# A one-core decoder trunk step: the S5 steps dealt out over nearly the whole body, and two attention-branch units ahead of the gated unit

## The chip, the cores and the metric

The kernel runs on one core of a Trainium2 chip. The metric is device time in microseconds (us) of one execution, the median of three runs. The core's engines each run a queue of their own in order: TensorE (PE, matrix products; PEld is its loading of weights), VectorE (DVE), ScalarE (ACT), GpSimd (POOL) and SyncE (SP), which here issues the transfers between the chip's main memory and the core's on-chip memory. Engines wait for each other by semaphores.

## The reference, cut

One layer of a hybrid decoder, for 256 prompt tokens and 8 x 8 sample tokens that share the weights; the kernel carries all 320 tokens together.

```python
h = rmsnorm(x)
z = h @ w_in                     # S5 input | GLA q, k, v, gate, forget | memory q | 3 x merge gates
y_s5, s5_state   = s5(u_s5)      # diagonal complex state space, scan over time, then
                                 # y = gelu(y);  y = y * sigmoid(y @ w_glu + b_glu)
y_gla, gla_state = gla(q, k, v, r, a_low, s0)   # 4 heads, chunked; per-head rmsnorm; * silu(r)
y_x              = memory_attention(q_x, mem_k, mem_v)   # 4 heads, 256 memory tokens
merged = gate0 * (y_s5 @ w_br_s5) + gate1 * (y_gla @ w_br_gla) + gate2 * (y_x @ w_br_xattn)
x = x + merged @ w_out
x = x + swiglu(rmsnorm(x))
y = rmsnorm(x)                   # returned with the new states and the memory's k and v
```

## The kernel before, in words

Every weight matrix is read in units of 128 x 2048 fp32 (1 MB). A unit is loaded by SP into one of three `raw` buffers (L70), rounded by ScalarE to `whi` (L82), and VectorE takes the remainder `wlo` (L83); both have two buffers. Activations are split in the same way into a high and a low part. `mm3` (L95) then makes three products for each block of 128 rows: high x high (L99), high x low (L100), low x high (L101), 48 matmuls of 128x320 in a unit. The names ending in h and l are such pairs: `hh, hl` the normed input, `yxh, yxl` the attention branch's output, `ygh, ygl` the GLA's, `ysh, ysl` the gated S5's, `y1h, y1l` the S5 output ahead of its gate.

The program has three stages. `front` norms the input and projects the memory (to about 100 us). `body` (L1082) makes the products with `w_in` and everything that hangs on them, and `back` (L1127) makes the merge, the output projection and the feed-forward part.

`body` runs three streams of steps, written as generators: `main` (four attention heads, then `IDLE` empty steps, `gla_setup` at L846, then four GLA heads, `gla` at L888), `s5` (eight tiles of the S5 scan: products `bu` at L658, tables and scans on VectorE up to L704, products `yp` at L713), and `gates` (48 units whose results go to `d_gate` by L1079). A stream has a number of steps and of units, `STEPS`, and an end, `ENDS`: its pace is (steps + units) / end, and the loop at L1110 always takes the stream that is furthest behind by its pace. So `ENDS` says at which share of the body a stream is done. Before, S5 has 0.8.

A GLA head ends as follows, and the places named below lie here. For each half of the sample tokens, SP loads four states into `gl_s` (L1016; one buffer), TensorE multiplies them (L1020), ScalarE copies (L1025), TensorE transposes (L1028), VectorE adds into `gl_o` (L1032), makes masked values `gl_vr` (L1040), TensorE multiplies (L1043), VectorE updates the states (L1046), and SP stores them (`o_gs`, L1050). After the second half: L1055, the head's sum of squares (L1061, L1062), its inverse root (TensorE L134, VectorE L142 to L154, TensorE L162), the scaling of `gl_o` (L1064), two units for the output gate (`gl_sr`, stored to `d_r`, L1070), and the store of the head to `d_yg` (L1072).

`back` first loads the attention output in four pieces (`yraw<-d_yx`, L1141, two buffers `yraw`) and splits them into `yxh, yxl` (L1124, L1125), then the GLA output (`yraw<-d_yg`, with `yr<-d_r`, L1147 to L1151) into `ygh, ygl`. The gated unit (GLU) comes next: four units of `w_glu` on `y1h, y1l`, which need the end of S5. Then `branch(m2, bi)` takes a unit of `w_br` for output pair m2 and branch bi (2 attention, 1 GLA, 0 S5): load of the gates `gld`, 48 matmuls, products with the gates into `macc`. The order before is (0,2), (1,2), (0,0), (1,0), (0,1), (1,1), then for each m2 from 2 to 7 the branches 2, 1, 0.

A scheduler turns this into one queue for each engine, so that steps of different streams, and of body and back, stand between each other on an engine; the orders shown below are those queues.

Of the kernel before, what the change touches and what calls it, by code (L numbers as in the profile page):

```python
# [8 lines left out]
F32 = mybir.dt.float32  # L9
F32R = mybir.dt.float32r  # L10
U8 = mybir.dt.uint8
I32 = mybir.dt.int32
AF = mybir.ActivationFunctionType
ALU = mybir.AluOpType
# [4 lines left out]
P = 128  # L19
# [3 lines left out]
NT = NP_ + NS  # L23
# [6 lines left out]
IDLE = 14  # L30
STEPS = (129 + IDLE, 32), (113, 8), (49, 48)
W_PROJ = 1.0
ENDS = (1.0, 0.8, 1.0)
HEADS = 4
FH = 5632
FQ = 4
# [8 lines left out]
C_BGLU, C_GN, C_BA, C_DS = 64, 72, 80, 84  # L45
# [4 lines left out]
class Build:  # L50
# [1031 lines left out]
    def body(self):  # L1082
        def s5():
            self.prepared = self.s5_prep(0)
            yield
            for ut in range(8):
                yield from self.s5_tile(ut, self.prepared)
# [5 lines left out]
        def main():  # L1093
            yield from heads(self.attn)

            for _ in range(IDLE):
                yield
            self.pop(self.left)
            self.pop(self.left)
            self.gla_setup()  # L1100
            yield from heads(self.gla)
# [5 lines left out]
            [it, (steps + W_PROJ * proj) / end, 0]  # L1107
            for it, (steps, proj), end in zip((main(), s5(), self.gates()), STEPS, ENDS)
        ]
# [17 lines left out]
    def back(self):  # L1127
        nc, io = self.nc, self.io
        TT = nc.vector.tensor_tensor
        self.wide = True  # L1130
        yp = self.push(self.left, "y", bufs=1)
# [3 lines left out]
        ys = []  # L1135
        for n, d in (("x", self.d_yx), ("g", self.d_yg)):
            hi = yp.tile([P, 8, NT], F32R, name=f"y{n}h")
            lo = self.low(yp, f"y{n}l", 8)
# [12 lines left out]
                    TT(raw[:], raw[:], r[:], op=ALU.mult)  # L1151
                self.split(hi[:, 2 * c : 2 * c + 2, :], lo[:, 2 * c : 2 * c + 2, :], raw[:])
            ys.insert(0, (hi, lo))
        hi = yp.tile([P, 8, NT], F32R, name="ysh")
        lo = self.low(yp, "ysl", 8)
        gp = self.push(self.right, "glu", bufs=1)
        y1h = gp.tile([P, 8, NT], F32R, name="y1h")
        y1l = self.low(gp, "y1l", 8)
        for c in range(2):
            nc.scalar.activation(  # L1160
                self.y1[:, 4 * c : 4 * c + 4, :], self.y1[:, 4 * c : 4 * c + 4, :], AF.Gelu_apprx_tanh
            )
        for m in range(8):
            self.split(y1h[:, m, :], y1l[:, m, :], self.y1[:, m, :])
        for m2 in range(4):
            wh, wl = self.unit(io["w_glu"][m2])
            for i in range(2):
                m = 2 * m2 + i
                ps = self.psum_mm()
                self.mm3(ps[:, :NT], wh, wl, 8 * i, 8, y1h, y1l)  # L1170
                sg = yp.tile([P, NT], F32, name="glu", tag="glu", bufs=2)
                nc.scalar.activation(sg[:], ps[:, :NT], AF.Sigmoid, bias=self.vec[:, C_BGLU + m : C_BGLU + m + 1])
                TT(sg[:], sg[:], self.y1[:, m, :], op=ALU.mult)
                self.split(hi[:, m, :], lo[:, m, :], sg[:])
        ys.insert(0, (hi, lo))
        gates = self.d_gate[:].rearrange("p (b m) t -> p b m t", b=3)
        self.pop(self.right)
        bp = self.push(self.right, "branch", bufs=1)
        acc = {}

        def branch(m2, bi, last=0):
            wh, wl = self.unit(io["w_br"][bi, m2])
            g = bp.tile([P, 2, NT], F32, name="gld", tag="gld", bufs=3)
            nc.sync.dma_start(g[:], gates[:, bi, 2 * m2 : 2 * m2 + 2, :])
            nc.scalar.activation(g[:], g[:], AF.Sigmoid)
            for i in range(2):
                m = 2 * m2 + i
                ps = self.psum_mm()
                self.mm3(ps[:, :NT], wh, wl, 8 * i, 8, *ys[bi])
                if bi == 2:  # L1190
                    acc[m] = bp.tile([P, NT], F32, name="macc", tag="macc", bufs=4)[:]
                    TT(acc[m], ps[:, :NT], g[:, i, :], op=ALU.mult)
                else:
                    TT(g[:, i, :], ps[:, :NT], g[:, i, :], op=ALU.mult)
                    TT(acc[m], acc[m], g[:, i, :], op=ALU.add)
                    if bi == last:
                        self.split(mh[:, m, :], ml[:, m, :], acc[m])


        for m2, bi in ((0, 2), (1, 2), (0, 0), (1, 0), (0, 1), (1, 1)):  # L1200
            branch(m2, bi, last=1)
        for m2 in range(2, 8):
            for bi in (2, 1, 0):
                branch(m2, bi)
# [25 lines left out]
        for m in range(KD):  # L1230
            wh, wl = self.unit(io["w_out"][m])
            ps = self.psum_mm()
# [13 lines left out]
        for q in range(FQ):  # L1246
            for i in range(FT):
                m = q * FT + i
                wh, wl = self.unit(io["w_fg"][m])
# [6 lines left out]
                wh, wl = self.unit(io["w_fu"][m])  # L1256
# [4 lines left out]
            for m in range(KD):  # L1261
                wh, wl = self.unit(io["w_fd"][q, m], FT * P)
                ps = self.psum_mm()
# [128 lines left out]
```

## Time and profile before

| | us |
|---|---|
| runs (three) | 2089.7, 2090.43, 2091.97; median 2090.43 |
| the profiled execution's own time | 2090.89 |
| its span, first to last instruction | 2089.1 |
| TensorE busy | 2064.1 (99%) |
| VectorE busy | 1290.8 (62%) |
| ScalarE busy | 852.2 (41%) |
| GpSimd busy | 141.2 (7%) |

The profile is one execution, and the time of its rows runs from 0 at the first instruction. Matmuls are pipelined, so the durations of single ones overlap and their starts tell the rate. In a row of a timeline, `[1.50 <-DMA gl_s<-s]` says that the engine was idle for 1.50 us before the instruction, and what ended that. The four GLU units run from 845.8 to 876.9 us, the first unit with `yxh` starts at 876.88.

### The profile page before, as it was taken

Reading aid. Unit: us, or ns where it says so; the run is one execution under the profiler, and the core shown is the slowest. Engines: PE = TensorE matmul, PEld = TensorE weight load, DVE = VectorE, ACT = ScalarE, POOL = GpSimd, SP = SyncE. Lnnn points to the kernel's source line nnn. Section 1 sums busy time; section 2 is a strip of 40 time slices with the busy share of each in tenths; the row PEclk is TensorE's granted clock in tenths of the full one; section 3 lists DMA queues with packets and bytes.
Section 4 is the critical chain, followed back from the end, with each engine's and each line's share of the span. In section 5 each row is a group of like instructions: output and inputs, shape, how many; then the busy total and the mean of one; then the engine's idle time right before and its main releaser. Section 6 shows DMA issues by size and latency. Waiting matters only on the chain.

```text
span 2089.1 us, 33964 instructions
## 1 busy us (share of the span) xinstructions
PE 2064.1 (99%) x14390; PEld 2014.3 (96%) x14390; DVE 1290.8 (62%) x1961; ACT 852.2 (41%) x1121; POOL 141.2 (7%) x181
## 2 busy tenths in 40 slices
PE   9999999999999999999999999999999999999997
PEld 7998998999999999999999999999999999999997
DVE  7977779887997945675555444444444444444445
ACT  7544445554445344544333333233323333333343
POOL 8211011012101000000000000000000000000000
PEclk9999999999999999999999999999999999999998
DMA  9765664445454454766554444454435443454443
GB/s 336 257 233 196 230 219 150 151 151 173 140 180 149 148 197 148 259 216 200 189 196 161 142 144 140 142 180 147 156 125 178 152 151 130 152 178 146 149 135 111
DMA packets 71673, 362.23 MB, mean 173 GB/s; under 512 B 8032, under 2 KB 16096, under 8 KB 41696
## 3 DMA queue, kind: packets, MB, share of 16 engines
q1 hardware_dynamic: 71520, 360.05, 50.3%
q8 instruction: 113, 1.85, 0.4%
q14 instruction: 40, 0.33, 0.0%
HBM read 338.49 MB, written 21.53 MB: 172 GB/s over the span
## 4 chain that ended last, share of the span: by engine, by line
PE 89%; DVE 7%; DMA 1%; issue 1%; ACT 1%; SPq 0%; DVEq 0%; ACTq 0%
PE pmm L101 19%; PE pmm L99 18%; PE pmm L100 18%; PE psm L101 10%; PE psm L99 10%; PE psm L100 9%; DVE wlo L83 2%; DVE s_w L677 1%; DMA o_gs<-gl_s 1%; DMA gl_s<-s 0%; PE psm L954 0%; ACT whi L82 0%; PE psm L805 0%; PE yp L713 0%; PE bu L658 0%
## 5 line engine op out<-in xcount | busy, mean ns | idle before, releaser
L82 ACT CAST whi<-raw 128x2048 fp32r<-128x2048 f32 (+3 forms) x308 | 540.2, 1754 | 931.5 <-issue 528.8
L83 DVE TENSOR_TENSOR wlo<-raw,whi 128x2048 fp32r<-128x2048 f32 (+3 forms) x308 | 646.1, 2098 | 279.5 <-ACT whi L82 277.7
L101 PE MATMUL pmm<-hh,wlo 128*128 128x320 f32 x1408 | 438.6, 311 | 2.9 <-DVE wlo L83 2.8
L99 PE MATMUL pmm<-hh,whi 128*128 128x320 f32 x1408 | 437.2, 311 | 0.0
L100 PE MATMUL pmm<-hl,whi 128*128 128x320 f32 x1408 | 432.3, 307 | 0.0
L99 PEld LDWEIGHTS pmm<-hh,whi 128*128 128x128 f32 x1408 | 265.5, 189 | 5.8 <-issue 5.5
L101 PEld LDWEIGHTS pmm<-hh,wlo 128*128 128x128 f32 x1408 | 264.4, 188 | 6.9 <-DVE wlo L83 3.5
L100 PEld LDWEIGHTS pmm<-hl,whi 128*128 128x128 f32 x1408 | 265.3, 188 | 2.0 <-issue 1.3
L101 PE MATMUL pmm<-fh,wlo 128*128 128x320 f32 x704 | 216.8, 308 | 0.0
L101 PE MATMUL psm<-fh,wlo 128*128 128x320 f32 x704 | 216.8, 308 | 0.0
L99 PE MATMUL psm<-fh,whi 128*128 128x320 f32 x704 | 215.5, 306 | 0.0
L99 PE MATMUL pmm<-fh,whi 128*128 128x320 f32 x704 | 215.5, 306 | 0.0
L100 PE MATMUL pmm<-fl,whi 128*128 128x320 f32 x704 | 213.4, 303 | 0.0
L100 PE MATMUL psm<-fl,whi 128*128 128x320 f32 x704 | 213.3, 303 | 0.0
L99 PEld LDWEIGHTS psm<-fh,whi 128*128 128x128 f32 x704 | 132.2, 188 | 0.1
L100 PEld LDWEIGHTS psm<-fl,whi 128*128 128x128 f32 x704 | 132.2, 188 | 0.0
L100 PEld LDWEIGHTS pmm<-fl,whi 128*128 128x128 f32 x704 | 132.2, 188 | 0.0
L99 PEld LDWEIGHTS pmm<-fh,whi 128*128 128x128 f32 x704 | 132.1, 188 | 0.0
L101 PEld LDWEIGHTS pmm<-fh,wlo 128*128 128x128 f32 x704 | 131.7, 187 | 0.0
L101 PEld LDWEIGHTS psm<-fh,wlo 128*128 128x128 f32 x704 | 131.6, 187 | 0.0
L101 PE MATMUL pmm<-hidh,wlo 128*128 128x320 f32 x352 | 108.9, 309 | 0.2 <-DVE wlo L83 0.2
L101 PE MATMUL psm<-hidh,wlo 128*128 128x320 f32 x352 | 108.4, 308 | 0.0
(448 smaller groups left out, 3648.6 us busy)
## 6 DMA issues: line engine op xcount, KB each, us to landing
raw<-w_in SPq DMA_DIRECT2D x88, 1024.0 KB, 4.9
raw<-w_fg SPq DMA_DIRECT2D x44, 1024.0 KB, 4.8
raw<-w_fu SPq DMA_DIRECT2D x44, 1024.0 KB, 4.8
raw<-w_fd SPq DMA_DIRECT2D x64, 704.0 KB, 4.1
raw<-w_br SPq DMA_DIRECT2D x24, 1024.0 KB, 4.9
at_kv<-kv SPq DMA_DIRECT2D x32, 512.0 KB, 5.7
raw<-w_out SPq DMA_DIRECT2D x16, 1024.0 KB, 4.9
raw<-w_mk SPq DMA_DIRECT2D x8, 1024.0 KB, 6.2
```

Source lines behind the costliest of these rows:

```text
L82: nc.scalar.copy(hi[:, s], raw[:, s])
L83: nc.vector.tensor_tensor(lo[:, s], raw[:, s], hi[:, s].bitcast(F32), op=ALU.subtract)
L99: nc.tensor.matmul(ps, hi[:, ws], xh[:, kx + k, :], start=k == 0, stop=False)
L100: nc.tensor.matmul(ps, hi[:, ws], xl[:, kx + k, :], start=False, stop=False)
L101: nc.tensor.matmul(ps, lo[:, ws], xh[:, kx + k, :], start=False, stop=k == nk - 1)
L677: nc.vector.tensor_tensor_scan(fl[:, c * n : c * n + m], af[:, :m], fl[:, c * n : c * n + m], 0.0, op0=M, op1=A)
```

## The change

Two edits. `ENDS` for the S5 stream goes from 0.8 to 0.93, so that its pace falls and its steps are dealt out over 93% of the body. In `back`, the GLU is put into a function and called after `branch(0, 2)` and `branch(1, 2)`; `ys[bi - 3]` finds the same pair, since at that time the list holds two or three pairs and is counted from its end. The pool "branch" is now taken before the pool "glu".

```diff
-ENDS = (1.0, 0.8, 1.0)
+ENDS = (1.0, 0.93, 1.0)
...
-        hi = yp.tile([P, 8, NT], F32R, name="ysh")
-        lo = self.low(yp, "ysl", 8)
-        gp = self.push(self.right, "glu", bufs=1)
...
-        ys.insert(0, (hi, lo))
         gates = self.d_gate[:].rearrange("p (b m) t -> p b m t", b=3)
-        self.pop(self.right)
         bp = self.push(self.right, "branch", bufs=1)
...
-                self.mm3(ps[:, :NT], wh, wl, 8 * i, 8, *ys[bi])
+                self.mm3(ps[:, :NT], wh, wl, 8 * i, 8, *ys[bi - 3])
...
-        for m2, bi in ((0, 2), (1, 2), (0, 0), (1, 0), (0, 1), (1, 1)):
+        def glu():
+            hi = yp.tile([P, 8, NT], F32R, name="ysh")
+            lo = self.low(yp, "ysl", 8)
+            gp = self.push(self.right, "glu", bufs=1)
...
+            ys.insert(0, (hi, lo))
+            self.pop(self.right)
+
+
+        branch(0, 2)
+        branch(1, 2)
+        glu()
+        for m2, bi in ((0, 0), (1, 0), (0, 1), (1, 1)):
             branch(m2, bi, last=1)
```

In the rows that follow, "waits" names the engines or transfer queues that an instruction waits for, and x2 stands for so many equal rows.

First place: TensorE at the end of the body, in the second half of the last GLA head (`gl_oi` is what L1020 gave, copied; L1028 transposes it). Before, its steps stand between products of a body unit, here those ahead of and behind the transposes; 23 such products lie between L1020 and L1028:

```order
L100 MATMUL pmm<-hl,whi 128x320
L1028 MATMUL psm<-ident,gl_oi 128x128 [waits Activation_49]
L1028 MATMUL psm<-ident,gl_oi 128x128
L1043 MATMUL psm<-gl_vr,gl_k_8467 128x256 x2
L101 MATMUL pmm<-hh,wlo 128x320
L99 MATMUL pmm<-hh,whi 128x320
L100 MATMUL pmm<-hl,whi 128x320
```

After, on the same engine, from L1020 to the row ahead of the attention branch's first product:

```order
L1020 MATMUL psm<-gl_s_9009,gl_qe 32x256 x2
L1028 MATMUL psm<-ident,gl_oi 128x128 [waits Activation_49]
L1028 MATMUL psm<-ident,gl_oi 128x128
L1043 MATMUL psm<-gl_vr,gl_k_8385 128x256 [waits DVE_49] x3
L1055 MATMUL psm<-gl_v,gl_kt 128x256 [waits PE_49]
L1055 MATMUL psm<-gl_v,gl_kt 128x256
L1043 MATMUL psm<-gl_vr,gl_k_8385 128x256 [waits DVE_49]
L134 MATMUL psm<-ones,nsum 128x1 [waits DVE_49]
L134 MATMUL psm<-ones,nsum 128x1 x2
L162 MATMUL psm<-ident,rs_out 128x128 [waits DVE_49,Activation_49]
L162 MATMUL psm<-ident,rs_out 128x128
L162 MATMUL psm<-ident,rs_out 128x64
```

The next row there is the first product with `yxh`. The products of units that stood between these steps are gone from between them: the body's last unit ends ahead of L1020.

Second place: SP at the same time. After the change, the loads of the attention output stand behind the store of the last head:

```order
L1050 DMA o_gs<-gl_s_9009 128x1024 [waits DMAHW0_49,DVE_49]
L1072 DMA d_yg<-gl_o 128x640 [waits DMAHW6_49,DVE_49]
L1141 DMA yraw<-d_yx 128x640 [waits DMAHW7_49,PE_49]
L1141 DMA yraw<-d_yx 128x640
L1144 DMA yr<-d_r 128x640 [waits DMAHW4_49,DMAHW1_49]
L1144 DMA yr<-d_r 128x640 [waits DMAHW2_49,PE_49]
L1141 DMA yraw<-d_yx 128x640 [waits DMAHW7_49,DMAHW3_49,DVE_49]
L1141 DMA yraw<-d_yx 128x640 [waits DMAHW0_49,DVE_49]
L1141 DMA yraw<-d_yg 128x640 [waits DMAHW5_49,DMAHW3_49,DVE_49]
```

Before, they stand in the same order, with loads of `w_br` between them:

```order
L1050 DMA o_gs<-gl_s_9009 128x1024 [waits DMAHW3_49,DMAHW2_49,DVE_49]
L1072 DMA d_yg<-gl_o 128x640 [waits DVE_49]
L1141 DMA yraw<-d_yx 128x640 [waits DMAHW4_49,PE_49]
L1141 DMA yraw<-d_yx 128x640 [waits DMAHW5_49]
L1144 DMA yr<-d_r 128x640 [waits DMAHW6_49,DMAHW0_49]
L1144 DMA yr<-d_r 128x640 [waits DMAHW7_49,PE_49]
L70 DMA raw<-w_br 128x2048 [waits DVE_49]
L1141 DMA yraw<-d_yx 128x640 [waits DMAHW4_49,DMAHW1_49,DVE_49]
```

What moved is not the loads but the work around them: the loads of `w_br` for the first two units now stand ahead of this piece.

Third place: VectorE at the GLA setup, from the subtractions L885 over the scans L886 to the next `wlo`. Before, with the S5 steps L664 and L665 between the scans:

```order
L885 TENSOR_TENSOR gl_mt<-gl_mt,gl_b 128x320
L886 SCALAR_TENSOR_TENSOR gl_b<-mask,gl_mt 128x320 [waits DVE_49]
L664 TENSOR_TENSOR s_w<-bu,s_tab 128x2x5x64 [waits PE_49]
L886 SCALAR_TENSOR_TENSOR gl_b<-mask,gl_mt 128x320 [waits DVE_49]
L665 TENSOR_TENSOR s5Q<-bu,s_tab 128x640
L886 SCALAR_TENSOR_TENSOR gl_b<-mask,gl_mt 128x320 [waits DVE_49] x2
L940 TENSOR_TENSOR gl_e<-gl_b 128x128 [waits DVE_49]
L83 TENSOR_TENSOR wlo<-raw,whi 128x2048 [waits DMAHW6_49,Activation_49]
```

After:

```order
L885 TENSOR_TENSOR gl_mt<-gl_mt,gl_b 128x320 x3
L886 SCALAR_TENSOR_TENSOR gl_b<-mask,gl_mt 128x320 [waits DVE_49] x4
L940 TENSOR_TENSOR gl_e<-gl_b 128x128 [waits DVE_49]
L941 TENSOR_TENSOR gl_e<-gl_b 128x128
L940 TENSOR_TENSOR gl_e<-gl_b 128x2x64
L941 TENSOR_TENSOR gl_e<-gl_b 128x2x64
L83 TENSOR_TENSOR wlo<-raw,whi 128x2048 [waits DMAHW6_49,PE_49,Activation_49]
```

The S5 steps have left this stretch, and three short steps of the first GLA head have come ahead of `wlo`.

## Rows read from the trace of the kernel before

**Rows 1.** The page: busy time of TensorE; VectorE's busy tenths in 40 slices.
```profile
PE 2064.1 (99%) x14390; PEld 2014.3 (96%) x14390; DVE 1290.8 (62%) x1961; ACT 852.2 (41%) x1121; POOL 141.2 (7%) x181
...
DVE  7977779887997945675555444444444444444445
```

**Rows 2.** The waits of TensorE: instruction, releaser: total us, times, longest us.
```profile
PE pmm L101 <- DVE wlo L83: 3.2, 3, 2.8
PE psm L1020 <- DMA gl_s<-s: 3.1, 2, 1.6
...
PE bu L658 <- DVE s5Q L665: 0.8, 1, 0.8
PE bu L658 <- issue: 0.7, 1, 0.7
PE psm L780 <- DVE at_p L763: 0.6, 1, 0.6
```

**Rows 3.** Windows: length, busy PE, PEld, DVE, ACT, POOL, granted clock, DMA.
```profile
374.00:377.00 3.00, 0.20 (x3) 0.05 (x1) 3.00 (x4) 1.68 (x2) 0.00 (x0) 1.00 0.02 5
...
378.00:381.20 3.20, 3.20 (x14) 3.20 (x13) 3.20 (x5) 0.00 (x0) 0.00 (x0) 0.52 0.83 294
...
1200.00:1240.00 40.00, 40.00 (x279) 40.00 (x278) 18.62 (x17) 12.52 (x12) 0.00 (x0) 1.00 0.42 141
```

**Rows 4.** The chain of waits from 820 to 864: start, us, what.
```profile
827.24 7.65 DMA o_gs<-gl_s
834.90 4.39 DMA gl_s<-s
```

**Rows 5.** Timeline of TensorE, then ScalarE, 838 to 860: start, us, instruction.
```profile
839.43 0.64 PE L1020 MATMUL psm<-gl_s,gl_qe 128*32 128x256 f32 x8 [1.50 <-DMA gl_s<-s]
...
843.45 0.38 PE L1028 MATMUL psm<-ident,gl_oi 128*128 128x128 f32 x2
...
848.96 0.72 PE L134 MATMUL psm<-ones,nsum 128*128 128x1 f32 x6
...
854.55 0.97 PE L162 MATMUL psm<-ident,rs_out 128*128 128x128 f32 x6
...
840.12 0.37 ACT L1025 COPY gl_oi<-psm 128x256 f32<-128x256 f32 x1 [1.81 <-PE psm L1020]
```

**Rows 6.** Landing times of L1050's stores, then of L1016's loads.
```profile
DMA to landing us min/median/max: 3.7/5.0/7.6
...
DMA to landing us min/median/max: 3.8/4.1/4.6
```

**Rows 7.** Timeline of VectorE, 839 to 860.
```profile
843.87 0.29 DVE L1032 TENSOR_TENSOR gl_o<-gl_o,psm 128x32 f32<-128x32 f32 x2 [3.56 <-PE psm L1028]
...
845.39 0.48 DVE L1062 TENSOR_TENSOR nsum<-gl_sq 128x320 f32<-128x320 f32 x1
...
850.06 0.87 DVE L1046 SCALAR_TENSOR_TENSOR gl_s<-gl_s,gl_eb,psm 128x256 f32<-128x256 f32 x2
850.84 0.15 DVE L142 TENSOR_SCALAR rs_v<-psm 128x3 f32<-128x3 f32 x1
...
852.82 0.16 DVE L154 SCALAR_TENSOR_TENSOR rs_out<-rs_t,rs_y 128x3 f32<-128x3 f32 x1
```

**Rows 8.** Timeline of SP, 805 to 880.
```profile
856.41 0.32 SPq L1072 DMA_DIRECT2D d_yg<-gl_o  x1
856.82 0.88 SPq L1141 DMA_DIRECT2D yraw<-d_yx  x2
```

**Rows 9.** The tile `yraw`: durations ns min/median/max, first and last start.
```profile
L1147 DVE SCALAR_TENSOR_TENSOR yraw<-yraw,vec,yr x8: 546/547/552, 876.5 to 893.0; 128x320 f32<-128x320 f32 x8
...
L1124 ACT CAST yxh<-yraw x4: 723/728/734, 861.7 to 870.6; 128x640 fp32r<-128x640 f32 x4
L1125 DVE TENSOR_TENSOR yxl<-yraw,yxh x4: 818/820/825, 864.1 to 871.5; 128x640 fp32r<-128x640 f32 x4
...
DMA to landing us min/median/max: 3.3/4.6/5.2
```

More of the change, by code (lines that the diff above doesn't have):

```diff
@@ L1153, in back @@
             ys.insert(0, (hi, lo))
-        hi = yp.tile([P, 8, NT], F32R, name="ysh")
-        lo = self.low(yp, "ysl", 8)
-        gp = self.push(self.right, "glu", bufs=1)
[L1157 to L1174, printed above, removed]
-        ys.insert(0, (hi, lo))
         gates = self.d_gate[:].rearrange("p (b m) t -> p b m t", b=3)
-        self.pop(self.right)
         bp = self.push(self.right, "branch", bufs=1)
@@ L1197, in branch @@
                         self.split(mh[:, m, :], ml[:, m, :], acc[m])
-        for m2, bi in ((0, 2), (1, 2), (0, 0), (1, 0), (0, 1), (1, 1)):
+        def glu():
+            hi = yp.tile([P, 8, NT], F32R, name="ysh")
+            lo = self.low(yp, "ysl", 8)
+            gp = self.push(self.right, "glu", bufs=1)
+            y1h = gp.tile([P, 8, NT], F32R, name="y1h")
+            y1l = self.low(gp, "y1l", 8)
+            for c in range(2):
+                nc.scalar.activation(
+                    self.y1[:, 4 * c : 4 * c + 4, :], self.y1[:, 4 * c : 4 * c + 4, :], AF.Gelu_apprx_tanh
+                )
+            for m in range(8):
+                self.split(y1h[:, m, :], y1l[:, m, :], self.y1[:, m, :])
+            for m2 in range(4):
+                wh, wl = self.unit(io["w_glu"][m2])
+                for i in range(2):
+                    m = 2 * m2 + i
+                    ps = self.psum_mm()
+                    self.mm3(ps[:, :NT], wh, wl, 8 * i, 8, y1h, y1l)
+                    sg = yp.tile([P, NT], F32, name="glu", tag="glu", bufs=2)
+                    nc.scalar.activation(sg[:], ps[:, :NT], AF.Sigmoid, bias=self.vec[:, C_BGLU + m : C_BGLU + m + 1])
+                    TT(sg[:], sg[:], self.y1[:, m, :], op=ALU.mult)
+                    self.split(hi[:, m, :], lo[:, m, :], sg[:])
+            ys.insert(0, (hi, lo))
[4 more added lines that the diff above has]
+        for m2, bi in ((0, 0), (1, 0), (0, 1), (1, 1)):
             branch(m2, bi, last=1)
```

## The prediction

> **What bounds the kernel now.** I read the page first: TensorE is busy 2064.1 us of a span of 2089.1 [rows 1], so only some 25 us are idle, and VectorE's tenths in 40 slices (52 us each) fall from 7 to 9 in slices 2 to 15 to 4 to 5 from slice 16 on [rows 1]. Next the list of what TensorE waited for [rows 2]: apart from the start and the end, it is a `wlo` once for 2.8 us, the state load `gl_s` twice (3.1 in all), and the S5 and attention steps (`s5Q` 0.8, issue 0.7, `at_p` 0.6). Then the windows [rows 3]: at steady state 279 matmuls take 40 us, 143.4 ns each at granted clock 1.00, and a unit of 48 is 6.9 us. The 2.8 us wait lies in 374 to 377, and after it 14 matmuls take 3.2 us at granted clock 0.52: 1.2 us lost on top. TensorE is thus the bound, its work does not change, and the time can move only by what TensorE waits, or by its clock.
>
> **Part 1, S5 over 93% of the body.** The S5 stream's pace falls from 121/0.8 = 151 to 121/0.93 = 130, so its VectorE work is thinner in the crowded first two thirds and reaches into the stretch where VectorE stood at 4 to 5 tenths. What it can give back is bounded by the waits that are there. At the GLA setup, two S5 steps and their `bu` products stood between the scans L886; in the order after, they are gone from there, and `wlo` comes sooner. By durations of the trace, VectorE does 8.9 us from one `wlo` to the next there, where it did 11.0; but 18.5 where it did 17.2 just ahead. I take the 2.8 us to fall to 0.5 [rows 2] and the 1.2 to 1.7 us of slow clock behind it (the matmuls between 377 and 378 are slowed too) to go: -2.3 and -1.5. The `gl_s` wait that is not the last head's: 14.7 us of TensorE work now lie over a store and load that had 11.4, so -1.6. `bu` twice and `at_p`: about -2 [rows 2]. In return S5 steps fall now on heads where VectorE had room, and I see two runs of units (44 to 50 and 78 to 81) in which VectorE has more to do than a unit's 6.9 us; they can cost 1 to 5, I take 2.4. Sum of part 1: -5, with ends -9 (nothing new waits) and +1 (the old waits only move).
>
> **Part 2, the start of the merge.** Before, the last S5 step lies some 100 us ahead of the body's end, so the GLU units (L134 and L162 between them) could fill TensorE while the last GLA head was finished by short dependent steps. In the order after, TensorE has nothing between L1020 of the last half and the first product of `yxh`: the last S5 step ends only two or three units ahead, the GLU comes behind two x units, and these need `yraw<-d_yx`, which stands on SP behind the store `d_yg` of that head, which waits for L1064. So the chain that was covered is now bare. Its terms:
>
> (a) The state's store and load. They took 7.65 + 4.39 [rows 4], and TensorE started L1020 at 839.43, 12.2 us after the store was issued [rows 5]. After the change, TensorE has 8.9 us of units left when the store can go out (the `wlo` of the last unit but one stands ahead of L1046 on VectorE and ends 4.3 us into that unit; 0.9 for L1046 follow; the two units with what stands between them end at 14.1). So 12.2 - 8.9 = 3.3 of waiting. Shortest landings of both lines, 3.7 + 3.8 [rows 6], would make it 0.
>
> (b) From L1020 to the store `d_yg`. L1020's start to the end of the copy L1025: 840.49 - 839.43 = 1.06 [rows 5]. The transposes L1028 to VectorE's L1032: 0.42 + 0.05 [rows 5, 7]. L1032's start to L1062's end: 2.0; behind it the second pair of L1046 (0.87) and L134 (0.72) [rows 5, 7], 3.6 together if in series. L142 to L154: 852.98 - 850.84 = 2.14 [rows 7], with 0.1 of handing over. L162's start to the store on SP: 856.41 - 854.55 = 1.86 [rows 5, 8]. Sum 9.2.
>
> (c) Store to first x product: SP 0.41 later [rows 8], the load 4.6 (3.3 to 5.2), the cast `yxh` 0.73 and a hand-over [rows 9]: 5.8. SP does not wait for the store to land.
>
> (b) and (c) are 15.1 us (13.3 to 15.9), in which TensorE has its own L1020 to L162 to do, some 3.6: idle 11.5.
>
> (d) `yraw` has two buffers, so the second pair of loads waits for the first pair's `yxl`: 0.82 + 0.3 + 4.6 + 0.73 = 6.4, against 32 matmuls of the first unit's first half that need only the first pair, 4.6: about 2 (0 to 3).
>
> (e) The third unit's `wlo`. It stands on VectorE behind L1147 to L1125 of the g branch, whose `yraw<-d_yg` loads go out only when the x casts are done, 7.3 after the first x product; landing at 11.9, then four L1147 (2.2), two L1151 and one `ygl` (2.5), two L1169 (1.0) and `wlo` (2.3) end at 19.9 [rows 9]. TensorE gets there at 13.9 + 2 + 0.3 = 16.2: about 3.5 (0 to 4.5).
>
> (f) The clock: the 3 us wait at 374 was followed by the half clock [rows 3], and here TensorE idles longer. 1.5 us would be lost, of which (d) hides a part: 1 (0 to 3.5).
>
> Sum 3.3 + 11.5 + 2 + 3.5 + 1 = 21.3. What goes: the `gl_s` wait of 1.5 at the same place [rows 5] and some 0.4 before the third GLU unit (what remains of L101's 3.2 beside 2.8 [rows 2]). Net +19, ends +11 and +25. Later units are the same products in another order, and TensorE is full there: nothing.
>
> A price from elsewhere: the `yraw` loads landed in 4.6 us in the middle [rows 9]. The Trainium skill, DMA: Bandwidth & Descriptors, section "Anatomy of one DMA — SWDGE (gpsimd) path", gives about 2.0 us fixed plus bytes over 436 GB/s, for another kind of issue than SP's; for 327,680 bytes that is an estimate of 2.75, and by it the three rounds in (c), (d) and (e) would be some 5.5 us shorter and the time about 2099. The measured landing decides.
>
> **The sum.** The profiled run took 2090.9, 0.5 over the median of three. 2090.4 - 5 + 19 = 2104.4, I say 2105. A measurement here tells 0.2% from no change, 4.2 us: slower is over 2094.6.
>
> **Rivals.**
> - Short transfers: the stretch has fewer weight loads than before, and every transfer lands at its shortest. (a) is 0, (c) 1.3 less, (d) 0.5, (e) 1.5, the clock stays up: +10 at the merge; with -8 in the body 2092 to 2093, not slower. It decides where store and load stay under 8.9 us together and `yraw` under 3.5. Against it: 12.2 in the same place [rows 4, 5] and a middle of 4.6 [rows 9]. 0.10.
> - The clock does not come back within the first x unit. At granted 0.52 [rows 3] a matmul is 143.4/0.52 = 276 ns; the two x units' 96 would take 12.7 us more, of which (d), (e) and the 1 of (f) hide 6.5: +6, 2111; through the third unit, 2117. For it: the waits (a) to (e) come in pieces, and one wait of 3 us already cost the clock [rows 3]. Against it: there it was back after 3.5 us of matmuls. The Trainium skill, TensorE: Matmul & The Clock Gate, section "HAM oscillation — how this bites in real kernels", says that matmuls in short groups between DMA waits start at the low clock group after group; what rows 3 show agrees for one group, and no row shows it for several. 0.16.
> - The change gives what a thinner S5 stream could at most, and the x units find their data ready because the scheduled order does not hold at run time: body -9, merge 0 to -2, about 2080. Against it: each engine runs its queue in order, and SP's `yraw` is behind `d_yg` there. 0.04.
>
> **How the numbers follow.** Forecast 0.70, with a range of its own of 2098 to 2111. The range for 8 in 10 leaves out most of the first rival, the third, and the clock's far end: 2094 to 2115. Faster by over 0.2%: 0.03 (the third rival, nearly all). Within 0.2%: 0.09 (the first rival, and 0.01 of the third's upper end, less what of the first lies above 2094.6). Slower: 0.88.
>
> **What would show it.** Right: TensorE's list of waits has `gl_s` about 3 us, then `psm` of L1028, L134 and L162 with VectorE and ScalarE as releasers, and L99 of `yxh` waiting 5 us for ScalarE behind a `yraw` load, together 13 to 16 us between 845 and 890; L101 waits for `wlo` some 3 us two units later; the waits at 374 us, for `bu` and for `at_p` are smaller; from the third merge unit on the two kernels run at one distance. Wrong, if the body keeps its waits or gets new ones over 5 us (part 1), if `yraw` lands in under 3.5 us, or if the granted clock stays near 0.5 over the x units (second rival).

## The result and the profile of the changed kernel

The changed kernel takes 2112.0 us (median of four runs, 2111.4 to 2113.1) against 2090.1 before: a ratio of 1.011, with a 95% interval of 1.010 to 1.012. The forecast was 2105 us with a range of 2094 to 2115, so the sign held, and the size was 7 us short: +22 instead of +14, outside the range of the forecast itself (2098 to 2111) and inside the wider one. TensorE does the same 14390 matmuls; it is idle for 40 us of the span instead of 25, and its busy time is 5 us longer. The page, with the lines that answer to [rows 1] (the last is the granted clock in 40 slices):

```profile
span 2109.6 us, 33959 instructions
...
PE 2069.5 (98%) x14390; PEld 2018.1 (96%) x14390; DVE 1288.4 (61%) x1961; ACT 852.3 (40%) x1120; POOL 128.4 (6%) x181
...
DVE  7967679696986887566655444444444444444445
...
PEclk9999999999999999799999999999999999999999
```

VectorE is busier in slices 15 and 16 than before (8 and 7 for 4 and 5), where the S5 steps now lie, and one slice shows a lower clock, the 17th: the start of the merge. To see what each half of the change did, I compare the start of the same unit's first product in both traces (timeline of TensorE). Before, for the unit behind the GLA setup, the last body unit, and the first unit behind the six that were exchanged:

```profile
385.29 0.31 PE L99 MATMUL pmm<-hh,whi 128*128 128x320 f32 x1
...
836.03 0.31 PE L99 MATMUL pmm<-hh,whi 128*128 128x320 f32 x1
...
904.78 0.31 PE L99 MATMUL pmm<-ygh,whi 128*128 128x320 f32 x1
```

And after the change, the same three:

```profile
378.38 0.31 PE L99 MATMUL pmm<-hh,whi 128*128 128x320 f32 x1
...
837.91 0.31 PE L99 MATMUL pmm<-hh,whi 128*128 128x320 f32 x1
...
925.50 0.31 PE L99 MATMUL pmm<-ygh,whi 128*128 128x320 f32 x1
```

Up to the setup the changed kernel is 6.9 us ahead (over half of that is S5 work on TensorE that comes later now: 12 of its products are not yet done; waits and half clock up to there account for 3.2). At the last body unit it is 1.9 behind. At the merge it loses another 18.8, and from there on both run at one distance. So the body gave +1.9 where the forecast had -5, outside its ends of -9 and +1, and the merge +18.8 where it had +19.

The list of TensorE's waits answers to [rows 2]:

```profile
PE psm L1020 <- DMA gl_s<-s: 11.0, 4, 5.7
PE pmm L99 <- ACT yxh L1124: 5.4, 1, 5.4
PE psm L162 <- DVE rs_out L154: 2.3, 1, 2.3
PE pmm L101 <- DVE wlo L83: 2.0, 4, 1.1
PE psm L877 <- DVE s_wb L605: 1.3, 1, 1.3
```

The wait of 2.8 us for `wlo` at the setup has shrunk to 1.1, where 0.5 was forecast, and a new one of 1.3 us for an S5 step (`s_wb`) stands beside it; the half clock behind the old wait is gone. The wait for `gl_s` has grown from 3.1 to 11.0 us. Of these, 5.2 are in three places in the body, where it was 1.6 in one: that is the larger part of what the forecast of the body missed.

The bare chain of the merge, in the timeline of TensorE (answers to [rows 5]):

```profile
850.73 1.08 PE L1020 MATMUL psm<-gl_s,gl_qe 128*32 128x256 f32 x8 [5.73 <-DMA gl_s<-s]
852.29 0.69 PE L1028 MATMUL psm<-ident,gl_oi 128*128 128x128 f32 x2 [0.48 <-ACT gl_oi L1025]
...
855.93 1.27 PE L134 MATMUL psm<-ones,nsum 128*128 128x1 f32 x6
859.54 1.81 PE L162 MATMUL psm<-ident,rs_out 128*128 128x128 f32 x6 [2.33 <-DVE rs_out L154]
...
866.74 0.64 PE L99 MATMUL pmm<-yxh,whi 128*128 128x320 f32 x1 [5.39 <-ACT yxh L1124]
...
884.11 0.41 PE L101 MATMUL pmm<-y1h,wlo 128*128 128x320 f32 x1 [0.49 <-DVE wlo L83]
```

Most steps of the last head wait for another engine, nothing stands between, and the same instructions take nearly twice as long as in [rows 5] (L1020 1.08 for 0.64, L162 1.81 for 0.97). The windows say why (the number ahead of the last two is the granted clock); the first one lies in the body, behind the longest wait for `gl_s` there:

```profile
730.40:734.00 3.60, 3.60 (x21) 3.19 (x22) 0.00 (x0) 0.37 (x1) 0.12 (x1) 0.64 0.99 405
...
844.00:851.00 7.00, 1.27 (x11) 0.98 (x14) 2.20 (x2) 2.85 (x3) 0.00 (x0) 0.75 0.76 238
851.00:856.00 5.00, 4.29 (x19) 2.83 (x12) 2.32 (x8) 1.11 (x2) 0.00 (x0) 0.50 0.83 270
856.00:861.00 5.00, 2.67 (x13) 2.39 (x12) 2.67 (x13) 0.37 (x1) 0.00 (x0) 0.50 0.41 164
861.00:867.00 6.00, 0.61 (x3) 0.42 (x3) 1.11 (x2) 0.76 (x2) 0.00 (x0) 0.50 0.67 209
867.00:871.00 4.00, 4.00 (x16) 4.00 (x17) 1.36 (x2) 1.05 (x2) 0.00 (x0) 0.50 0.79 244
871.00:875.00 4.00, 4.00 (x28) 4.00 (x27) 1.65 (x2) 1.10 (x2) 0.00 (x0) 0.96 0.36 102
```

From 851 to 871 the clock stands at half, 1.2 GHz, also for the first 4 us of the x unit's products (16 matmuls where 28 fit).

What happened in the body shows in the chain of waits, here at 717 us:

```profile
715.15 2.20 DVE wlo L83
717.36 0.79 DVE gl_s L1046 x2
...
718.17 8.24 DMA o_gs<-gl_s
...
726.42 3.77 DMA gl_s<-s
...
730.33 0.64 PE psm L1020 x8
```

and SP's timeline at the same place:

```profile
717.38 0.33 SPq L70 DMA_DIRECT2D raw<-w_in  x1
718.17 0.34 SPq L1050 DMA_DIRECT2D o_gs<-gl_s  x1
```

When `wlo` ends at 717.35, a `raw` buffer is free, and SP issues the next weight load, 1 MB; the state update L1046 stands right behind `wlo` on VectorE, so the store of the states goes out 0.8 us after that load, and lands 8.24 us later. In the kernel before, at the same step of the same head, two S5 steps (L701, L702) stood on VectorE between `wlo` and L1046:

```profile
725.80 2.28 DVE L83 TENSOR_TENSOR wlo<-raw,whi 128x2048 fp32r<-128x2048 f32 x1
728.01 0.81 DVE L701 TENSOR_TENSOR s5R<-s_w,s_tab 128x640 f32<-128x640 f32 x1
728.75 0.81 DVE L702 TENSOR_TENSOR s5Q<-s_w,s_tab 128x640 f32<-128x640 f32 x1
729.48 0.86 DVE L1046 SCALAR_TENSOR_TENSOR gl_s<-gl_s,gl_eb,psm 128x256 f32<-128x256 f32 x2
```

There the store followed the load by 2.25 us (728.12 and 730.37 on SP) and landed in 4.0. For the other first halves, whose store the next load of states waits for, the distance fell from 2.58 to 1.36 us, from 3.18 to 0.78 and, at the last head, from 1.04 to 0.78, and the landing went from 3.7 to 5.8 us, from 4.2 to 6.4 and from 7.65 to 9.8.

### The profile page after: what moved, and what is told of

Read it like the earlier page. It is cut to its first block, busy times and chain, and to the rows that moved or that the text cites. A ratio compares the mean times of both kernels' runs of the same rounds, so it can differ in the third digit from the quotient of the medians.

```text
span 2109.6 us, 33959 instructions
## 1 busy us (share of the span) xinstructions
PE 2069.5 (98%) x14390; PEld 2018.1 (96%) x14390; DVE 1288.4 (61%) x1961; ACT 852.3 (40%) x1120; POOL 128.4 (6%) x181
## 4 chain that ended last, share of the span: by engine, by line
PE 89%; DVE 5%; DMA 3%; ACT 2%; issue 1%; SPq 0%; DVEq 0%; ACTq 0%
PE pmm L101 18%; PE pmm L99 18%; PE pmm L100 18%; PE psm L101 10%; PE psm L99 10%; PE psm L100 9%; DMA o_gs<-gl_s 1%; DVE wlo L83 1%; DMA gl_s<-s 1%; ACT whi L82 1%; DVE s_w L677 1%; PE psm L954 1%; PE bu L658 0%; PE yp L713 0%; DMA yraw<-d_yx 0%
```

## The experiments

The eleven kernels were timed in three rounds, each beside the kernel before on one chip; times are medians. Two settings are varied in most of them, the end of S5 and the order of the merge, and a third, the number of buffers for `gl_s`, was added to test the stores.

**S5's end alone.**

```diff
-ENDS = (1.0, 0.8, 1.0)
+ENDS = (1.0, 0.93, 1.0)
```

> Only the S5 stream's end goes from 0.8 to 0.93; the merge keeps the gated unit first. Theory M (the loss comes from the merge order: with the gated unit behind two x units nothing stands beside the last GLA head's end): TensorE has products of the gated unit between L1020 and L162 again, the merge costs as before, and only the body's +2 us remains: 2092 us (2089 to 2095). Rival S (the later end of S5 alone takes the cover away, since the gated unit then waits for the last S5 step): 2100 to 2110.

Measured: 2096.7 against 2089.8, ratio 1.003 (1.002 to 1.004), between the two theories and nearer to M. In the profiled run (2095.45), even with the gated unit first, the last body unit's start is 0.8 us later than before, and 4 more are lost at the merge: in its order products of the gated unit stand around L1020 to L1055, but none between L134 and L162. The timeline of TensorE has one wait there:

```profile
856.54 1.81 PE L162 MATMUL psm<-ident,rs_out 128*128 128x128 f32 x6 [2.55 <-DVE rs_out L154]
```

and the windows have the half clock behind it:

```profile
857.00:861.00 4.00, 4.00 (x16) 3.66 (x16) 1.71 (x3) 0.46 (x1) 0.00 (x0) 0.50 0.26 82
861.00:865.00 4.00, 4.00 (x23) 4.00 (x22) 0.00 (x0) 0.95 (x1) 0.00 (x0) 0.75 0.98 318
```

So the end of S5 is not free with the old merge, but it is the smaller part. The body's order is that of the changed kernel, with the same distances between store and load, and its three places wait 3.1 us for `gl_s`, not 5.2: so much can one execution differ from another.

**The merge order alone.** The changed kernel with `ENDS` at 0.8.

> Only the order of the merge is changed (two x units ahead of the gated unit); the S5 stream ends at 0.8 as before. In its order one body unit stands between L1020 and L1028, and nothing from there to the first product of yxh. Theory M: some 11 us of waiting and 4 to 6 us of half clock, less the 2 us lost there before: 2105 us (2100 to 2110). Rival S: the gated unit's input is ready early, the merge costs nothing more than before: 2090 to 2093.

Measured: 2103.1 against 2089.8, ratio 1.007 (1.005 to 1.008). Theory M: with S5 done earlier by some 100 us, as in the kernel before, the merge still waits (5.0 us for `yxh`, 4.4 ahead of L162), since the gated unit stands behind the x units in TensorE's queue whether it could run or not. The two edits alone cost 6.9 and 13.2; together 22.

**Two buffers for the states.** In the changed kernel:

```diff
-            s0 = gp.tile([P, SB // 2, 256], F32, name="gl_s0", tag="gl_s0", bufs=1)
+            s0 = gp.tile([P, SB // 2, 256], F32, name="gl_s0", tag="gl_s0", bufs=2)
```

> The changed kernel with two buffers for the state halves gl_s instead of one, so that the load of the second half no longer waits for the store of the first. Theory D (the waits for gl_s, 11.0 us in four places, come from the store's landing of 8 to 10 us in series with the load): they go, with the slow clock behind that of 730 us; the bare chain of the merge stays: 2098 us (2095 to 2102). Rival: the transfers were slow because the queues were full, and the load is late in any order: 2106 to 2112.

Measured: 2097.1, ratio 1.004 (1.002 to 1.005); inside theory D's range, and 15 us less than the changed kernel. The first product of the last body unit starts at 832.3 us: 3.7 ahead of the kernel before, where the changed kernel was 1.9 behind. But the second buffer changed the order as well: the last half's steps from L1020 to L134 now stand between products of body units, and TensorE waits only 0.25 us ahead of L162. What is left is one long wait at the merge. The timeline:

```profile
824.92 0.64 PE L1020 MATMUL psm<-gl_s,gl_qe 128*32 128x256 f32 x8
...
841.49 1.04 PE L162 MATMUL psm<-ident,rs_out 128*128 128x128 f32 x6 [0.25 <-DVE rs_out L154]
```

and in the list of waits:

```profile
PE pmm L99 <- ACT yxh L1124: 10.0, 1, 10.0
```

So the 15 us are the store in series and a changed merge together. What the series alone cost in the changed kernel is read from its list of waits, 11.0 us and the slow clock behind the longest in the body.

**Matmuls that keep the clock up.** `spin` adds fp32 products into a PSUM tile that S5 no longer uses:

```diff
+    def spin(self, x, n):
+        bu = self.pbu.tile([P, 2, 512], F32, name="bu", tag="bu", bufs=1)
+        for _ in range(n):
+            self.nc.tensor.matmul(bu[:, 0, : x.shape[-1]], self.ident[:], x, start=True, stop=True)
...
+            if h == HEADS - 1 and half == 0:
+                self.spin(s0[:, 3, :], 11)
...
+        if h == HEADS - 1:
+            self.spin(o[:, 0, :], 8)
```

(and 4 with `nsum` ahead of L162; the lines of this kernel are numbered differently, but L162 is the same).

> The changed kernel with 23 additional fp32 matmuls, whose results nobody reads, put where TensorE waits at the end of the body: 11 ahead of L1020, 4 ahead of L162, 8 ahead of the first x product. They add work that should fit into the waits. Theory C (half clock costs 6 us there: 2.3 in the chain's own TensorE steps, 2 in the first x unit, the rest beside waits): the granted clock stays at 1.00 between 850 and 872 us and the time falls by 4 to 5 us to 2107.5. Rival (the slow clock only fills waits that would be there anyway): 2111 to 2114.

Measured: 2113.2, ratio 1.011 (1.010 to 1.013): nothing gained. The additional products held the clock at 1.00 up to 851 and again from 864, but not between:

```profile
852.00:856.00 4.00, 2.49 (x9) 2.11 (x8) 2.92 (x8) 0.83 (x2) 0.00 (x0) 0.61 0.59 181
856.00:860.00 4.00, 4.00 (x13) 3.02 (x12) 2.67 (x13) 0.28 (x1) 0.00 (x0) 0.50 0.71 283
860.00:864.00 4.00, 3.09 (x10) 2.09 (x9) 0.82 (x1) 0.00 (x0) 0.00 (x0) 0.61 0.00 0
864.00:868.00 4.00, 4.00 (x15) 2.89 (x16) 0.00 (x0) 0.66 (x1) 0.00 (x0) 1.00 0.82 235
```

and the four products ahead of L162 overran their place: at half clock they took 4.62 us, where TensorE had waited 2.33 us, though `rs_out` was ready at 859.28:

```profile
856.96 4.62 PE L170 MATMUL bu<-nsum,ident 128*128 128x320 f32 x8
861.37 1.68 PE L162 MATMUL psm<-ident,rs_out 128*128 128x128 f32 x6
```

So the chain from L1020 to the store `d_yg` was slower than in the changed kernel, 13.8 us for 11.5, the loads of the attention output went out 1.7 us later, and the x unit starts at 868.1, 1.4 later. At full clock its first product is 6.5 us ahead of the next unit's, instead of 8.9, but the units behind then wait more for their data (1.17 us for `wlo` where it was 0.49): from the first x product to the third GLU unit it is 30.7 us in this run and 30.9 in the changed kernel. So the half clock in the x unit covers waits that are there anyway. What the half clock costs in the chain the run can't tell, since the clock didn't hold there; theory C's condition was not met.

**The attention output's loads ahead of the head's store.**

```diff
-        nc.sync.dma_start(self.d_yg[:, 2 * h : 2 * h + 2, :], o[:])
+        q = nc.gpsimd if h == HEADS - 1 else nc.sync
+        q.dma_start(self.d_yg[:, 2 * h : 2 * h + 2, :], o[:])
```

> The changed kernel with the last head's store d_yg issued by GpSimd's queue, so that on SP the loads of d_yx no longer stand behind it. Theory B (these loads wait only for their place in SP's queue): they go out right after the store of the states, some 5 us sooner, TensorE's wait of 5.4 us for yxh falls to 1 or less: 2107 us (2105 to 2109). Rival G (what the x units gain is given back two units later, where the third unit's wlo waits for the g branch's loads and casts): 2110 to 2112.

Measured: 2108.5, ratio 1.009 (1.007 to 1.010), 3.5 less than the changed kernel. The loads go out at 856.1 instead of 862.7, and the wait for `yxh` falls to 2.6, not to 1: issued 0.4 us behind the store of the states, the first two loads land later than before (in 5.6 and 5.9 us, 3.3 and 3.9 in the changed kernel). Of the 6.5 us the merge keeps 2.6. The time is inside theory B's range, but the wait fell only by half, and `wlo` is waited for 1.1 us at the third unit instead of 0.5, as rival G has it.

**A quarter of the store.**

```diff
-            nc.sync.dma_start(io["o_gs"][h, :, hb], s0[:])
+            nc.sync.dma_start(io["o_gs"][h, :, hb][:, 3:], s0[:, 3:])
```

> The changed kernel, but each store o_gs writes only the last of its four states (128 KB of 512; the other states of the output are left out), issued at the same place. Theory Q (the store waits behind the 1 MB weight load that SP issued 0.8 us before, and its own bytes are the smaller part): where it landed in 8 to 10 us it lands in 5 to 6, the waits for gl_s fall from 11.0 to some 4 us: 2105 us (2103 to 2108). Rival W (store and load share the engines evenly, and the time is the store's own bytes): landing 2 to 3 us, no waits for gl_s left: 2098 to 2101.

Measured: 2107.4, ratio 1.009 (1.007 to 1.010). With 128 KB instead of 512 the landing at the last head falls from 9.8 to 7.2 us, at 718 from 8.2 to 6.6 (but 7.0 in three other kernels with whole stores and this order), at 588 from 6.4 to 4.7. The chain has the first of these:

```profile
837.52 7.17 DMA o_gs<-gl_s
```

So three quarters of the bytes are worth some 2 us; the larger part is what stands ahead of the store. That speaks for Q and against W, though the waits fell only to 8.0 us, and not to 4. They fell at the last head alone, from 5.7 to 2.3; in the body they are 5.7 for 5.2, since in this kernel's order less work stands between the store and L1020: 5.9, 8.5 and 7.6 us where it was 8.4, 10.3 and 8.8.

The traces of all kernels with whole stores, but for the one with added matmuls, say the same together (eleven kernels, eight stores each, read from SP's timeline and the landing lines of the store; the landing by the time since the nearest weight load ahead was issued):

| the nearest weight load was issued | stores | landing, us: lowest, median, highest |
|---|---|---|
| 0.6 to 0.9 us before | 19 | 6.1, 7.0, 9.8 |
| 0.9 to 1.6 | 28 | 4.9, 5.8, 8.2 |
| 1.6 to 2.7 | 24 | 3.4, 4.5, 7.7 |
| over 2.7 | 17 | 2.6, 3.4, 4.4 |

In the first three rows, 71 stores, the store always landed after the load ahead of it, 0.9 to 2.8 us behind it and in 49 of them less than 1.4. The load is slower too: it landed in 5.9 us (median) in the first row and in 5.2 in the third.

**Two buffers in the kernel before, and with S5 at 0.93 and the old merge.**

> The kernel before with two buffers for gl_s. Its two waits for gl_s (3.1 us) go and nothing else changes: 2086.5 us (2085 to 2088). If the earlier loads collide with weight loads: 2089 to 2091.

> S5 ending at 0.93, the gated unit first as before, and two buffers for gl_s. In its order units stand between L134 and L162 again. Theory P (the thinner S5 stream saves its 3 to 5 us in the first half of the body, and what it lost later was the store in series with the load): 2085 us (2082 to 2087), at or below the kernel before with two buffers. Rival N (the thinner stream brings new waits of its own): 2089 to 2094.

Measured: 2086.5 (ratio 0.9987, 0.998 to 0.9996) and 2084.2 (0.997, 0.996 to 0.998). The second is in theory P's range: with two buffers, the later end of S5 saves 2.3 us instead of costing 6.9, and the kernel beats both of the case. No wait for `gl_s` is in either list. But against one buffer at 0.93 (2096.7) only some 5 of the 12.5 us are the waits for `gl_s` and the half clock in the body (3.2 and 1.7). Another 6 are the wait of 2.55 us ahead of L162 and the half clock behind it, which are gone because units stand between L134 and L162 in this order.

**Two buffers with the new merge at 0.8, two with the old merge at 0.87, and one at 0.87.**

> The new merge order with S5 ending at 0.8, and two buffers for gl_s. In its order body units stand beside L1028 to L134; bare are only L162, L1064, the store d_yg and the loads behind it. Theory M (the merge order costs the store and load of the attention output whatever the S5 stream does): some 8 to 10 us of waiting for yxh and 2 us of half clock over the kernel before with two buffers (2086.5): 2097 us (2094 to 2100). Rival S (with S5 early there is work to stand beside it): 2087 to 2090.

> S5 ending at 0.87, the gated unit first, two buffers for gl_s. Theory P (the gain comes from the thinner S5 stream, and grows with its end): between the 2086.5 at 0.8 and the 2084.2 at 0.93, 2084 to 2087. Rival N (at each end other steps meet by chance, and the end is no lever by itself): outside, below 2083 or above 2088.

> S5 ending at 0.87, the gated unit first, one buffer for gl_s as before. Theory Q (what 0.93 loses with one buffer is the store that goes out 0.8 us behind a weight load, and the last GLA head's end without units beside it): in the order of 0.87 units stand between L134 and L162, so the merge costs as before, and the body gains or loses up to 3 us by where its stores fall: 2088 us (2085 to 2092). Rival E (a later S5 end costs in proportion): 2093 to 2095.

Measured: 2099.2 (1.004, 1.003 to 1.006), 2082.1 (0.996, 0.995 to 0.997) and 2083.6 (0.997, 0.996 to 0.998). The first is M: body units stand beside most of the chain now, and the one long wait is for `yxh`, 7.5 us. The other two ran ahead of what was expected: 0.87 is faster than 0.8 with one buffer and with two, and faster than 0.93 with one. With two, the 2 us to 0.93 are not clear of noise (the intervals of the two ratios overlap). The time lies below P's range and where N put it: the gain does not grow with the end. With one it lies 1.4 below Q's range, on Q's side. In the list of waits of the kernel with one buffer at 0.87, `gl_s` stands with 0.5:

```profile
PE psm L968 <- DVE gl_att L963: 1.6, 2, 1.2
...
PE psm L1020 <- DMA gl_s<-s: 0.5, 1, 0.5
```

Its stores went out 1.4 to 2.0 us behind a weight load in five of eight places. But the landings are only one part. First, more work lies over a store and load at 0.87: 9.5 to 10.7 us, and they take 8.4 to 11.1; at 0.93 with the same merge it is 8.4 to 10.9, and they take 8.7 to 10.9. Second, of the 12.4 us between the two profiled runs, `gl_s` and the half clock behind it are some 4; about 6 lie at the merge (the wait ahead of L162 and the half clock there), and 2 at the GLA setup, where TensorE waits 2.4 us at 0.93 and 0.5 at 0.87. So the end of S5 acts by which steps of the other streams come to stand beside which. What share of it is the meeting of store and load was not isolated, and why 0.87 comes out best was not tried further. All the times in one table (each beside its own runs of the kernel before, 2089.6 to 2090.4):

| merge, buffers for `gl_s` | S5 ends at 0.8 | 0.87 | 0.93 |
|---|---|---|---|
| gated unit first, 1 | 2090.1 (before) | 2083.6 | 2096.7 |
| x units first, 1 | 2103.1 | | 2112.0 (changed) |
| gated unit first, 2 | 2086.5 | 2082.1 | 2084.2 |
| x units first, 2 | 2099.2 | | 2097.1 |

The merge order costs 13 to 15 us in every column and row that has both.

## Why the prediction was right, and where it was short

**The direction and the merge: right.** Nothing stands between L1020 and the first x product, and TensorE waits there. The merge cost 18.8 for 19 forecast, but the terms did not fall as they were sized:

| term | forecast | measured | where it is read |
|---|---|---|---|
| (a) store and load of the states | 3.3 | 5.7 | wait ahead of L1020; landings 9.78 + 4.91 for 7.65 + 4.39 |
| (b) L1020 to the store `d_yg` | 9.2 | 11.5 | 850.73 to 862.23 |
| (c) to the first x product | 5.8 | 4.5 | to 866.74; the load took 3.86, not 4.6 |
| (d), (e) second loads, third `wlo` | 5.5 | about 1 | the units behind take 7.3, 7.7 and 7.0 us for 6.9 |
| (f) clock, in the first x unit | 1 | 2 | 866.74 to 875.64, for 6.9 |

(a) was short by the landings, since the work over them was sized right (9.2 us for 8.9). (b) was too short because its TensorE steps were taken at full clock, from rows in which other products kept it up; bare, they run at half clock. With TensorE's own 3.6 us of work taken off (b) and (c), the measured terms make 21 us, and 19 after the 2 us that the kernel before lost there. (d) and (e) were too long for two reasons: the loads behind the first pair landed in 2.8 to 4.1 us, not 4.6, and at half clock in the x unit there was more time for them (in the run with added products, at full clock there, the four units from the first x product on took 3.1 us more than 6.9 each, hardly less than the 3.3 here). So the mechanism of the merge is right, and that its sum came out within 0.2 us is luck: the errors cancel. The waits between 845 and 890 us make 14.7, in the 13 to 16 that were named as a sign of being right; the 3 us wait for `wlo` two units later came out at 0.5.

The second rival's time, 2111, is nearer to the 2112.0 than the forecast's 2105, but its condition was not met: the clock fell, and came back at some 871 us, within the first x unit, which runs from 866.7 to 875.6. The time came from the body instead. The Trainium skill (TensorE: Matmul & The Clock Gate, "HAM oscillation — how this bites in real kernels") says that matmuls in short groups between DMA waits start at the low clock group after group; the windows show it here for the whole chain, 851 to 871 us at 0.50, where TensorE's waits are for ScalarE and VectorE.

The estimate of 2.75 us for a `yraw` load, from the price that the Trainium skill gives for another kind of issue (DMA: Bandwidth & Descriptors, "Anatomy of one DMA — SWDGE (gpsimd) path"), was too short for SP's queue here too: they landed in 2.8 to 4.5 us. The first rival fell with the store and load of the last head, which took 14.7 us together where it needed under 8.9.

**The body: wrong.** The step that failed is the `gl_s` term of part 1: "14.7 us of TensorE work now lie over a store and load that had 11.4, so -1.6". It counted the cover at one head, and took the landing of the store as given. At that head the cover did grow, from 7.2 to 10.3 us between the store and L1020, but store and load grew from 8.8 to 10.9. At the two heads ahead of and behind it, which had not waited before, the cover shrank by 0.8 and 0.5 us, and store and load grew by 1.8 and 3.9. S5's steps on VectorE had also kept the store apart from the weight load. With them gone, L1046 stands directly behind `wlo` at the second and third head, the store follows the load by 0.8 us, and lands in 6.4 and 8.2 us, where in the kernel before it took 4.2 and 4.0. So the waits for `gl_s` in the body grew to 5.2 us instead of going (3.1 to 4.4 in the three other kernels with this order, one buffer and whole stores), with the half clock behind the longest (21 matmuls in 3.6 us at 0.64 from 730.4 on). This is a new wait of over 5 us, which the prediction had named as a sign that part 1 is wrong. Of its other terms, the half clock at the setup went as forecast (-1.7 for -1.5); `wlo` gave 1.7 for 2.3, and the new wait for `s_wb` took 1.3 of that back; `bu` gave 1.2 and `at_p` grew by 0.2, for 2 forecast; the 2.4 us for crowded units did not show as waits. That a thinner S5 stream saves something in the body is right: 2.3 us with two buffers at 0.93, and 6.8 at 0.87 without any second buffer.

That store and load in series are what TensorE waits for is shown by the list of waits and by two buffers, with which all waits for `gl_s` go. That the distance to the weight load sets the landing rests on its course in 88 stores; an experiment that changes the distance alone was not made. At the last head the distance hardly changed (1.04 to 0.78 us) and the landing still grew from 7.65 to 9.8, so why it was longest there stays open.

**The third rival** (that the queues would not hold) fell, as forecast: SP's loads stood behind the store, and moved up when the store was taken from that queue.

## What to carry to other kernels

When work is dealt out more evenly over an engine, look not only at what the engine will have to do but at what it kept apart: two transfers that are released by neighbouring instructions of one engine will go out together once the steps between them move away. When a second buffer or another pace makes a kernel faster, compare the orders too: here each such change also moved units beside short chains. Before an order of units is changed, ask for each short dependent chain which long work stands beside it in the queue; work that is ready but stands behind does not help. And price a bare chain at the low clock, its matmuls and the first microseconds behind it.

## What the runs showed that was not expected

A 512 KB store that SP issues 0.6 to 0.9 us after a 1 MB load lands in 7.0 us (median of 19), and in 3.4 (median of 17) when no load stands within 2.7 us ahead of it; a quarter of the bytes saves at most 2.6 us. When the load is issued less than 2.7 us ahead, the store lands 0.9 to 2.8 us behind it. And 23 additional matmuls did not keep the clock up in a chain that waits for other engines between its steps: it was granted 0.50 to 0.61 between 852 and 864 us, and four of them, put into a wait of 2.3 us, took 4.6 at that clock and made the chain longer.
